# ACT copies the attention sums out of PSUM, and DVE takes their reciprocal out of SBUF in two halves

## The chip, the cores and the metric

The kernel runs on one core of a Trainium2 chip. The time is device time in microseconds (us) of one execution; lower is better. The engines are PE (matrix products), DVE (vector), ACT (activations and copies), POOL (a second, slower vector engine) and SP, whose queue issues the kernel's DMA transfers. PE writes its results to PSUM, which DVE and ACT can read; POOL and the DMAs here work on SBUF and on main memory.

## The reference

One layer of a bidirectional encoder is computed for two sequences, `prompt` (1024 tokens) and `sample` (2048 tokens), with the same weights. Three groups of heads work beside each other on one input projection; the change lies in the two that are attention.

```python
def block_self_attention(q, k, v):          # 8 heads of 64, keys shared by 4 heads
    def one_block(qblk):
        s = jnp.einsum('bqkgd,bskd->bkgqs', qblk, k) * scale
        p = jax.nn.softmax(s, axis=-1)
        return jnp.einsum('bkgqs,bskd->bqkgd', p, v)
...
def memory_attention(q, k, v):              # 4 heads, 256 memory tokens
    s = jnp.einsum('bthd,bmhd->bhtm', q, k) * (D ** -0.5)
    p = jax.nn.softmax(s, axis=-1)
    return jnp.einsum('bhtm,bmhd->bthd', p, v)
...
    mix = jnp.concatenate([pool_out, attn_out, x_out], axis=-1)   # each times its silu gate
    y = jnp.einsum('bte,ed->btd', mix, w_out)
    return x + rms_norm(y, norm_post)
```

All values are float32.

## The kernel before

A first stage (up to about 700 us) normalises the inputs, makes the projections and writes q, k, v and gates to main memory. The second stage is attention, output projection and final norm; the change is in it.

**Groups.** The second stage takes 256 queries at a time, a `Pair`: eight pairs of `sample`, then four of `prompt`. Each pair has three `Group`s: kind 0 and kind 1 are self-attention over all keys (16 chunks of 128 keys in sample, 8 in prompt), kind 2 is attention over the memory (2 chunks). Their order is 0, 2, 1 (2, 0, 1 in the first pair): 36 groups, the last three of them after all others of the prompt.

**Slots.** The main loop runs over `slots`, one for each chunk of each group. In a slot, PE makes the scores of a chunk in two halves into S (`weights`, two PSUM buffers), ACT takes their exponential into P, DVE (and in sample POOL for the first 512 columns) adds P up over the chunks into z (`sums`), and `largest` looks ahead: it makes scores of a later group into a PSUM tile N, and DVE reduces that to its maximum. Products of P with V go into one PSUM tile `acc` (`values`, four chunks at a time), and pieces of the output projection of an earlier pair fill gaps on PE.

**The end of a group.** `at(slot, f)` puts work into a slot: with a whole number it stands between the two halves of `weights`, with + END (0.5) at the slot's end. Say that the group's last chunk is over and count the slots behind it as k = 0, 1, 2 and so on; they are those of the next groups.
- end of k=1, `totals`: PE adds z over the partitions, into a tile `zt` of the same pool as N. This pool (`psn`) has two buffers.
- k=2, `take`: DVE multiplies `acc` with the gate, into o.
- end of k=2, `inverse`: DVE takes the reciprocal of `zt` into rz; SP sends four rows of rz to main memory (`rows`) and then back, spread over 64 partitions each, as gz (two transfers).
- end of k=5 at the earliest, `mix_out`: POOL multiplies o by gz. Two slots' order later (k=7, between the halves) ACT rounds it into `mix`, and at the end of k=7 POOL makes the low part of `mix`. In a pair's kind-1 group this comes at once; for its other two groups a hold (`HOLD`) puts it many slots later.

**What sets the order.** PE, ACT, DVE and POOL run the instructions in the order in which this code issues them. SP's queue is not in that list: the scheduler puts the transfers in order. Every queue is worked off in its order, and an instruction that waits holds all behind it. Where each N stands is also decided when the kernel is built: the two buffers alternate, but in k=2 and k=3 behind each `zt` two tiles of `largest` follow each other in the one that `zt` does not hold, and that of k=4 comes into `zt`'s.

Line numbers: `largest` reduces N in line 194 and multiplies in 183 and 191; scores S are 220 and 224, their exponential 227; sums 239 (POOL) and 240 (DVE); values 252; totals 260; take 266; reciprocal 272; `rows` 274; gz 278; POOL's product o 288; `mix` 416; the transpose of the maxima 128 and the four small transfers of its rows into qb 209.

Of the kernel before, what the change touches and what calls it, by code (L numbers as in the profile page):

```python
# [7 lines left out]
F32 = mybir.dt.float32  # L8
# [15 lines left out]
def encoder(ctx, tc, I, O):  # L24


    nc = tc.nc
# [105 lines left out]
    class Group:  # L133
# [132 lines left out]
            nc.vector.tensor_tensor(out=self.o, in0=self.acc,  # L266
                                    in1=self.gate.rearrange("p i t q -> p (i t q)"), op=ALU.mult)

        def inverse(self):

            r = dbl.tile([128, 256], F32, name="rz", tag="rz", bufs=1)
            nc.vector.reciprocal(out=r, in_=self.zt[:, 0:256])  # L272
            rows = dram.tile([4, 256], F32, name="rows", tag="rows", bufs=4)
            nc.sync.dma_start(out=rows, in_=r[0:128:32])
            self.gz = dbl.tile([128, 512], F32, name="gz", tag="gz")
            for j in range(2):
                src = rows[2 * j:2 * j + 2].rearrange("l q -> (l q)").unsqueeze(0)
                nc.sync.dma_start(out=self.gz[64 * j:64 * j + 64], in_=src.broadcast_to([64, 512]))
# [13 lines left out]
    class Pair:  # L292
# [15 lines left out]
        def pool(self, slot):  # L308
            self.mix = [own.tile([128, NC, 2, 128], F32R, name="mix", tag=f"mix{hl}") for hl in range(2)]
            store_mix(slot, self, 0, self.u.rearrange("p c q -> p (c q)"),  # L310
                      self.g.rearrange("p c t q -> p (c t q)"))
# [96 lines left out]
    END = 0.5  # L408

    def at(slot, f, *args):  # L410

        later.setdefault(slot, []).append((f, args))
# [24 lines left out]
    for g in groups:  # L437
        n, c = first[g], g.chunks
        at(n + END, g.load_late)
        for k in range(0, c, RUN):  # L440
            ks = list(range(k, min(k + RUN, c)))
            at(n + ks[-1] + 1 + END, g.values, ks)
        at(n + c + 1 + END, g.totals)
        at(n + c + 2, g.take)
        at(n + c + 2 + END, g.inverse)
    for c in range(NC):
        at(4 + 3 * c, load_w_out, c)
        at(7 + 3 * c, split_w_out, c)
# [4 lines left out]
    looks, n = {}, len(slots)  # L453
# [406 lines left out]
    dbl = pool("p2two", 2)  # L860
# [14 lines left out]
    with tc.manual_schedule(engines=order):  # L875
        slot = 0
        while slot < len(slots) or later or fill:
            g, k = slots[slot] if slot < len(slots) else (None, 0)
# [13 lines left out]
            n = -(-(len(fill) - pauses) // max(1, until[0] - slot - pauses)) if fill else 0  # L892
            for _ in range(n):
                x = fill.pop(0)
                if x is None:
                    break
                out, h, c, start, final = x
# [57 lines left out]
```

## Time and profile before

| | us |
|---|---|
| median of 3 runs | 1884.36 |
| lowest and highest | 1883.71, 1887.12 |
| profiled execution, its own time | 1885.09 |
| profiled execution, span | 1883.0 |
| PE busy in the span | 1816.8 |
| DVE, ACT, POOL busy | 1131.4, 697.3, 856.7 |

The profile gives one execution. "Busy" is the time in which an engine runs instructions; a wait is idle time of an engine just before an instruction, put down to what ended it. The granted clock of PE is 1.00 at full speed and 0.50 at half; its mean here is 0.991. In a timeline row stand start, duration, engine, line, operation and tiles, and in brackets the idle time before it with what ended it; "x2" is two merged instructions.

### The profile page before, as it was taken

How to read it: one execution, taken by the hardware profiler on the slowest of the kernel's cores; microseconds unless marked ns; L12 is line 12 of the kernel's file. 1: busy time of each engine (PE TensorE's matmuls, PEld its weight loads, DVE VectorE, ACT ScalarE, POOL GpSimd, SP SyncE). 2: the span in 40 equal slices, each digit the busy share in tenths (PEclk: the TensorE clock that was granted, in tenths of full speed). 3: DMA queues.
4: the chain of work that ended last, by engine and by line, in shares of the span. 5: the costliest groups of instructions: out<-in, count | busy, mean ns of one | idle time of the engine just before them, and what ended most of it. 6: DMA issues, size and time to landing. Idle time of an engine off the chain costs nothing. (4 is left out here: it accounts for less than half of the span.)

```text
span 1883.0 us, 23531 instructions
## 1 busy us (share of the span) xinstructions
PE 1816.8 (96%) x8520; PEld 1282.0 (68%) x8520; DVE 1131.4 (60%) x1304; ACT 697.3 (37%) x1266; POOL 856.7 (45%) x756
## 2 busy tenths in 40 slices
PE   7999999999999998999999999999999999999996
PEld 6888888988988874465564656556565656565564
DVE  7755146431545167867768676767868576756743
ACT  5523233222422115434434343444434343433331
POOL 3665017520546008845638374664837461413313
PEclk9999999999999999999999999999999999999998
DMA  7634454254433926212122220212222242223211
GB/s 243 201 113 121 109 160 132 76 162 110 116 113 102 216 70 167 68 30 79 46 79 62 70 64 25 79 45 79 62 74 62 67 132 64 91 84 100 86 40 62
DMA packets 148485, 181.83 MB, mean 97 GB/s; under 512 B 21505, under 2 KB 118417, under 8 KB 148369
## 3 DMA queue, kind: packets, MB, share of 16 engines
q1 hardware_dynamic: 148368, 180.33, 33.6%
q8 instruction: 67, 1.10, 0.3%
q14 instruction: 50, 0.40, 0.1%
HBM read 126.50 MB, written 53.62 MB: 96 GB/s over the span
## 5 line engine op out<-in xcount | busy, mean ns | idle before, releaser
L227 ACT ACTIVATE P<-S 128x512 f32<-128x512 f32 x688 | 399.3, 598 | 558.3 <-PE S L220 436.2
L194 DVE TENSOR_REDUCE nb<-N 128x1 f32<-128x1024 f32 x256 | 311.6, 1218 | 240.3 <-PE N L191 239.5
L239 POOL TENSOR_TENSOR z<-z,P 128x512 f32<-128x512 f32 x224 | 316.9, 1415 | 223.7 <-ACT P L227 218.8
L252 PE MATMUL acc<-P,V 128*64 128x512 f32 (+1 forms) x1472 | 320.8, 578 | 0.5
L220 PE MATMUL S<-qa,KA 128*128 128x512 f32 x640 | 275.0, 430 | 9.2 <-ACT P L227 9.2
L240 DVE TENSOR_TENSOR z<-z,P 128x512 f32<-128x512 f32 (+1 forms) x272 | 273.6, 1006 | 12.7 <-ACT P L227 12.3
L63 POOL TENSOR_TENSOR rs<-rs,mhalf 128x1 f32<-128x1 f32 (+2 forms) x100 | 100.4, 1007 | 386.2 <-DVE rs L61 386.1
L220 PE MATMUL S<-qb,KB 65*128 65x512 f32 x640 | 254.5, 398 | 0.0
L548 PE MATMUL pz<-hT_hi,w_hi 128*128 128x512 f32 x592 | 233.2, 394 | 1.4 <-ACT vmst L806 0.8
L549 PE MATMUL pz<-hT_lo,w_hi 128*128 128x512 f32 x592 | 232.3, 392 | 0.0
L550 PE MATMUL pz<-hT_hi,w_lo 128*128 128x512 f32 x592 | 232.1, 392 | 0.2 <-DVE w_lo L69 0.2
L191 PE MATMUL N<-KA,qa 128*128 128x512 f32 x640 | 208.1, 406 | 18.4 <-DVE rz L272 11.7
L252 PEld LDWEIGHTS acc<-P,V 128*64 128x64 f32 x1472 | 98.6, 138 | 180.3 <-issue 171.2
L220 PEld LDWEIGHTS S<-qa,KA 128*128 128x128 f32 x640 | 120.4, 188 | 143.6 <-issue 72.5
L194 DVE TENSOR_REDUCE top<-N 128x1 f32<-128x1024 f32 (+1 forms) x88 | 107.0, 1218 | 96.7 <-PE N L191 76.9
L191 PEld LDWEIGHTS N<-KA,qa 128*128 128x128 f32 x640 | 116.9, 191 | 61.7 <-DVE nb L194 22.1
L548 PE MATMUL pz<-w_hi,hT_hi 128*128 128x384 f32 (+1 forms) x416 | 140.3, 338 | 1.4 <-ACT hT_hi L68 1.4
L549 PE MATMUL pz<-w_lo,hT_hi 128*128 128x384 f32 (+1 forms) x416 | 139.9, 336 | 1.0 <-DVE w_lo L69 0.9
L550 PE MATMUL pz<-w_hi,hT_lo 128*128 128x384 f32 (+1 forms) x416 | 140.1, 338 | 0.0
L357 PE MATMUL py<-wo_hi,mix 128*128 128x512 f32 x352 | 137.7, 391 | 0.0
L358 PE MATMUL py<-wo_lo,mix 128*128 128x512 f32 x352 | 137.6, 391 | 0.0
L359 PE MATMUL py<-wo_hi,mix 128*128 128x512 f32 x352 | 137.4, 390 | 0.0
(116 smaller groups left out, 2487.9 us busy)
## 6 DMA issues: line engine op xcount, KB each, us to landing
wraw<-w_in SPq DMA_DIRECT2D x15, 1536.0 KB
dg<-gst SPq DMA_DIRECT2D x48, 256.0 KB
qa<-dq SPq DMA_DIRECT2D x48, 256.0 KB
gz<-rows SPq DMA_DIRECT2D x72, 128.0 KB
x<-x_sample SPq DMA_DIRECT2D x16, 512.0 KB
xr<-x_sample SPq DMA_DIRECT2D x16, 512.0 KB
y_sample<-xr SPq DMA_DIRECT2D x16, 512.0 KB
dq<-qst SPq DMA_DIRECT2D x96, 64.0 KB
```

The source lines that it names most:

```text
L191: nc.tensor.matmul(S[:, 512 * b:512 * b + 512], lhsT=q, rhs=KA[self.kind][:, k:k + 512], start=True, stop=True)
L194: nc.vector.tensor_reduce(out=out, in_=S, axis=AX.X, op=ALU.max, negate=True)
L220: nc.tensor.matmul(S, lhsT=K[self.kind][rows_, keys], rhs=q, start=n == 0, stop=n == 1)
L227: nc.scalar.activation(out=self.P[k][:, j], in_=S, func=AF.Exp)
L239: nc.gpsimd.tensor_tensor(out=z[:, :cut], in0=a[:, :cut], in1=P[:, :cut], op=ALU.add)
L240: nc.vector.tensor_tensor(out=z[:, cut:], in0=a[:, cut:], in1=P[:, cut:], op=ALU.add)
L252: nc.tensor.matmul(self.acc[64 * j:64 * j + 64, x], lhsT=v, rhs=P[:, j, x], start=(k, i) == (0, 0), stop=k == self.chunks - 1, skip_group_ ...
L357: nc.tensor.matmul(ps, lhsT=mh, rhs=wo_hi[:, c, cols], start=first, stop=False)
L358: nc.tensor.matmul(ps, lhsT=mh, rhs=wo_lo[:, c, cols], start=False, stop=False)
L548: nc.tensor.matmul(ps, lhsT=sh, rhs=mh, start=c == 0, stop=False)
L549: nc.tensor.matmul(ps, lhsT=sh, rhs=ml, start=False, stop=False)
L550: nc.tensor.matmul(ps, lhsT=sl, rhs=mh, start=False, stop=c == n - 1)
```

## The change

`inverse` is cut in two. A new step `take_sums` in k=2 has ACT copy the 128 x 256 sums out of `zt` into an SBUF tile zs. At the end of k=2 DVE takes the reciprocal of the first 128 columns out of zs, and at the end of k=3 that of the other 128. Only then `rows` and gz are sent. zs and rz have one buffer each.

```diff
-        def inverse(self):
-
-            r = dbl.tile([128, 256], F32, name="rz", tag="rz", bufs=1)
-            nc.vector.reciprocal(out=r, in_=self.zt[:, 0:256])
+        def take_sums(self):
+
+            self.zs = dbl.tile([128, 256], F32, name="zs", tag="zs", bufs=1)
+            self.rz = dbl.tile([128, 256], F32, name="rz", tag="rz", bufs=1)
+            nc.scalar.copy(out=self.zs, in_=self.zt[:, 0:256])
+
+        def inverse(self, half):
+
+            r, t = self.rz, self.zs
+            x = slice(128 * half, 128 * half + 128)
+            nc.vector.reciprocal(out=r[:, x], in_=t[:, x])
+            if half == 0:
+                return
             rows = dram.tile([4, 256], F32, name="rows", tag="rows", bufs=4)
             nc.sync.dma_start(out=rows, in_=r[0:128:32])
...
         at(n + c + 1 + END, g.totals)
         at(n + c + 2, g.take)
-        at(n + c + 2 + END, g.inverse)
+        at(n + c + 2, g.take_sums)
+        at(n + c + 2 + END, g.inverse, 0)
+        at(n + c + 3 + END, g.inverse, 1)
```

With it the built program lets the two buffers of N alternate throughout: the tile of k=2 stands beside `zt`, that of k=3 in `zt`'s buffer, that of k=4 again in the other. PE's and POOL's own order is unchanged.

DVE, behind a kind-1 group of the prompt; z are the sums, N the look-ahead's scores, top and rows the maxima and their transpose. Before:

```order
L266 TENSOR_TENSOR o<-acc,gate 128x512
L272 RECIPROCAL rz<-N 128x256
L240 TENSOR_TENSOR z<-z,P 128x1024
L194 TENSOR_REDUCE top_5434<-N 128x4
L128 STREAM_TRANSPOSE rows_13825<-top_5434 128x32
L240 TENSOR_TENSOR z<-z,P 128x1024
```

And with the change (its lines behind 272 have moved by up to 11):

```order
L266 TENSOR_TENSOR o<-acc,gate 128x512
L279 RECIPROCAL rz<-zs 128x128
L240 TENSOR_TENSOR z<-z,P 128x1024
L194 TENSOR_REDUCE top_5434<-N 128x4
L128 STREAM_TRANSPOSE rows_13909<-top_5434 128x32
L279 RECIPROCAL rz<-zs 128x128
L240 TENSOR_TENSOR z<-z,P 128x1024
```

The second half stands behind a sum, a reduction and, here, the transpose.

SP's queue at the same place; qb<-rows are the four small transfers of the transposed maxima. Before:

```order
L173 DMA gate<-dg_1_3_74 128x2x128 x2
L274 DMA rows<-rz 4x256
L278 DMA gz<-rows 64x512 x2
L209 DMA qb<-rows_13825 1x8x32 x4
L209 DMA qb<-rows_13870 1x8x32 x4
```

With the change:

```order
L173 DMA gate<-dg_1_3_74 128x2x128 x2
L209 DMA qb<-rows_13909 1x8x32 x4
L283 DMA rows<-rz 4x256
L287 DMA gz<-rows 64x512 x2
L209 DMA qb<-rows_13960 1x8x32 x4
```

`rows` and gz now stand behind the first four of these transfers. So it is behind the kind-1 groups of the last sample pair and of the first three prompt pairs; behind the other sample pairs' kind-1 groups no transfer has changed its place.

ACT behind the same group, P<-S being exponentials, two to a slot. Before:

```order
L416 CAST mix<-o 128x512 x2
L227 ACTIVATE P<-S 128x512 x14
L416 CAST mix<-o 128x512
L227 ACTIVATE P<-S 128x512 x5
L365 COPY y<-py 128x512
```

With the change:

```order
L425 CAST mix<-o 128x512 x2
L227 ACTIVATE P<-S 128x512 x4
L273 COPY zs<-N 128x256
L227 ACTIVATE P<-S 128x512 x10
L425 CAST mix<-o 128x512
L227 ACTIVATE P<-S 128x512 x5
```

The copy stands after the first exponential of k=2; the rounding of `mix` for this group stands where it stood, ten exponentials later.

## Prediction

> **What bounds the kernel now.** I began with the page's busy shares, then read who waits for whom on the tensor engine, and then the order of time around single groups.
>
> ```profile
> PE 1816.8 (96%) x8520; PEld 1282.0 (68%) x8520; DVE 1131.4 (60%) x1304; ACT 697.3 (37%) x1266; POOL 856.7 (45%) x756
> ```
>
> PE is the bound: 66 us of the 1883.0 us span are all it does not work. A change that touches DVE and ACT can bring only what PE waits for them. For the buffers N, which `largest` and `totals` share, that is:
>
> ```profile
> PE N L191 <- DVE rz L272: 11.7, 13, 2.0
> PE N L191 <- DVE nb L194: 5.8, 16, 1.0
> PE N L183 <- DVE top L194: 2.1, 4, 0.6
> ...
> PE N L191 <- DVE rz L272: 5.2, 9, 0.6
> ...
> PE N L191 <- DVE rz L272: 5.9, 3, 2.0
> PE N L183 <- DVE top L194: 1.8, 3, 0.6
> ```
>
> The columns are us in total, times, longest. The first three rows are the whole run, the fourth is 700 to 1550 us (sample; all of the nb row falls there too), the last two 1580 to 1800 us (prompt). Together 19.6 us, 1.04% of the run; no more than that can be won from idle PE. I count slots from the end of a group: k=0 is the first slot of the group behind it. In k=2 and k=3 both `largest` tiles must use the one N that `zt` does not hold (the nb and top waits), and the one of k=4 waits for the reciprocal (rz). Of the nb row about 1.1 us (its longest and one of 0.2) lie elsewhere. So the sample groups offer 5.2 + 4.7 = 9.9 us, the last sample group 0.6 + 0.3 = 0.9, three of the prompt's four kind-1 groups 5.9 + 1.8 = 7.7 (behind the fourth there is no group).
>
> **The work itself.**
>
> ```profile
> L272 DVE RECIPROCAL rz<-N 128x256 f32<-128x256 f32 x36 | 62.9, 1748 | 4.4 <-PE N L260 3.6 <-DMA rows<-rz 0.8
> L609 ACT COPY z<-pz 128x256 f32<-128x256 f32 x24 | 9.3, 386 | 0.0
> ```
>
> The change adds 36 ACT copies. The trace has the same form, PSUM to SBUF: 386 ns, 13.9 us in all, on an engine that is 37% busy. A half reciprocal out of SBUF is not in the trace. Below, half of 1748 is 874 ns; above, a whole one. 6.8 ns an element says that the time is in the elements, so I take 0.9 us: DVE loses 36 x 0.05 = 2 us, off the path. Both ends matter little: at 1.7 us each DVE would lose 30 us of its 750 idle.
>
> **Sample groups: a gain.** A kind-1 group, k=2 to k=8, engine by engine:
>
> ```profile
> 909.65 1.75 DVE L272 RECIPROCAL rz<-N 128x256 f32<-128x256 f32 x1
> 911.31 0.63 DVE L240 TENSOR_TENSOR z<-z,P 128x512 f32<-128x512 f32 x1
> 911.86 1.21 DVE L194 TENSOR_REDUCE nb<-N 128x1 f32<-128x1024 f32 x1
> ...
> 907.49 0.60 ACT L227 ACTIVATE P<-S 128x512 f32<-128x512 f32 x1 [0.69 <-PE S L220]
> 919.35 1.19 ACT L227 ACTIVATE P<-S 128x512 f32<-128x512 f32 x2 [0.29 <-PE S L220]
> 920.43 0.61 ACT L416 CAST mix<-o 128x512 fp32r<-128x512 f32 x1
> ...
> 916.71 1.29 POOL L288 TENSOR_TENSOR o<-o,gz 128x512 f32<-128x512 f32 x1 [3.63 <-DMA gz<-rows]
> ...
> 909.19 0.73 PE L191 MATMUL N<-KA,qa 128*128 128x512 f32 x2 [0.31 <-DVE nb L194]
> 911.45 0.73 PE L191 MATMUL N<-KA,qa 128*128 128x512 f32 x2 [0.60 <-DVE rz L272]
> 921.64 0.47 PE L220 MATMUL S<-qa,KA 128*128 128x512 f32 x1
> ...
> 862.61 0.73 PE L191 MATMUL N<-KA,qa 128*128 128x512 f32 x2 [0.36 <-DVE nb L194]
> ```
>
> The copy stands behind the exponential of 907.49: done at 908.1 + 0.4 = 908.5, before the N of k=3 could start (909.19 - 0.31 = 908.9). That N now goes into zt's buffer, the next one into the buffer that L194 cleared at 909.1; both waits go, 0.91 us. The copy falls into ACT's pauses; without them it would cost at most 36 x 0.4 us.
>
> What comes later is gz. The second half stands behind L240 and L194: 909.65 + 0.9 + 0.6 + 1.2 + 0.9 - overlaps = 913.1, where the whole one ended at 911.4. So `rows`, gz and POOL's o move by 1.7 us, to 918.4; o ends at 919.7. ACT's mix, pulled ahead with PE to 919.5, waits 0.2, and the exponential behind it holds the S of 921.64 (now 920.7) by 0.15. A kind-1 group keeps 0.76 of 0.91 us; a kind-2 group keeps its 0.36 (last row), since its o comes many slots after its gz. Seven kind-1 groups lose 7 x 0.15 = 1.1: the sample side gains 9.9 - 1.1 = **8.8 us**. Bounds: 0, if ACT is late with the copy, to 9.9.
>
> **Prompt groups: the gain goes, and more may.** The order shows that in the last four kind-1 groups before the final one (one sample, three prompt) the four transfers qb<-rows now stand ahead of `rows` on SP. The first prompt one:
>
> ```profile
> 1632.20 0.69 DVE L266 TENSOR_TENSOR o<-acc,gate 128x512 f32<-128x512 f32 x1 [1.28 <-POOL mix L416]
> 1632.81 1.75 DVE L272 RECIPROCAL rz<-N 128x256 f32<-128x256 f32 x1
> 1636.80 0.21 DVE L128 STREAM_TRANSPOSE rows<-top 128x32 f32<-128x32 f32 x1
> ...
> 1630.97 0.74 PE L183 MATMUL N<-KA,qa 128*128 128x256 f32 x4 [0.59 <-DVE top L194]
> 1634.61 0.73 PE L191 MATMUL N<-KA,qa 128*128 128x512 f32 x2 [1.97 <-DVE rz L272]
> 1646.53 0.39 PE L224 MATMUL S<-qa,KA 128*128 128x256 f32 x2
> ...
> 1634.58 0.56 SPq L274 DMA_DIRECT2D rows<-rz  x1
> ...
> 1639.89 1.62 POOL L288 TENSOR_TENSOR o<-o,gz 128x512 f32<-128x512 f32 x1 [6.49 <-DMA gz<-rows]
> ...
> 1645.12 0.61 ACT L416 CAST mix<-o 128x512 fp32r<-128x512 f32 x1
> ...
> L209 SPq DMA_DIRECT2D qb<-rows x144: 623/632/791, 688.5 to 1795.5; - x144
> ```
>
> DVE's take is held by POOL (1.28), not by PE, so this chain keeps its place in time. The transpose ends 0.85 earlier, at 1636.2; four issues of 0.63 and the pauses between them take SP to 1638.95; then `rows`, 4.4 us later than 1634.58. From `rows` to o passed 5.3 us: o starts at 1644.3, ends at 1645.6 to 1645.9, and the mix moves from 1645.12 to 1645.9. PE has by then won 2.6 us and stands still for it: the exponential behind the mix ends at 1647.0, the S of 1646.53 starts then. The 2.6 us are gone and 0.5 is lost. With the same 4.4 us the other three follow from:
>
> ```profile
> 1568.43 1.29 POOL L288 TENSOR_TENSOR o<-o,gz 128x512 f32<-128x512 f32 x1 [11.39 <-DMA gz<-rows]
> 1715.27 1.27 POOL L288 TENSOR_TENSOR o<-o,gz 128x512 f32<-128x512 f32 x1 [8.07 <-DMA gz<-rows]
> 1788.87 1.27 POOL L288 TENSOR_TENSOR o<-o,gz 128x512 f32<-128x512 f32 x1 [6.87 <-DMA gz<-rows]
> ...
> 1571.39 0.61 ACT L416 CAST mix<-o 128x512 fp32r<-128x512 f32 x1
> 1719.92 0.61 ACT L416 CAST mix<-o 128x512 fp32r<-128x512 f32 x1
> 1794.86 0.61 ACT L416 CAST mix<-o 128x512 fp32r<-128x512 f32 x1
> ```
>
> o would end at 1574.1, 1720.9 and 1794.5: the mix moves by +2.7, +1.0 and -0.4; less 0.3 of slack as in the first, PE by +2.4, +0.7, -0.7. The four sum to **+2.9 us**; bounds: -8.6 (nothing is late, 0.9 and 7.7 are won) to +8 (o another 1.3 us later in each, a quarter of the 5.3 from `rows` to o).
>
> **The clock.**
>
> ```profile
> 1632.07:1635.48 3.41, 1.45 (x7) 0.82 (x5) 3.28 (x3) 1.08 (x2) 1.33 (x2) 1.00 0.88 282
> 1635.48:1638.89 3.41, 3.41 (x10) 0.99 (x10) 3.38 (x5) 0.60 (x1) 0.00 (x0) 0.50 0.32 99
> 1703.75:1707.16 3.41, 2.11 (x10) 1.16 (x9) 2.13 (x3) 2.17 (x4) 3.41 (x3) 1.00 0.49 171
> 1707.16:1710.57 3.41, 2.17 (x6) 1.33 (x8) 3.40 (x3) 0.06 (x1) 0.04 (x1) 0.50 0.70 212
> ```
>
> Stretches of 3.41 us, PE busy first, granted clock in the third column from the right: after one with PE busy for 1.45 or 2.11 of 3.41 the next is granted half. The old waits paid that before the mix, where it now lies under the wait. The new one, over 2 us without work, is paid behind it: 3.41 us at half clock is 1.5 to 1.7 us, 1.5 to 2.6 a group with a second stretch partly idle. I take 1.5, as behind 1635.48: 4 x 1.5 = **+6.0 us** (0 to 10.4). The Trainium skill, "TensorE: Matmul & The Clock Gate", Part 1, has half rate come after at least one idle window of about 3.4 us. The rows above, halved with PE busy for 42% and 62% of the window, speak against waiting for a whole one.
>
> The tail stays: its `rows` come after both halves back to back, 0.1 us later, beside PE work that lasts longer.
>
> **The sum.** -8.8 + 2.9 + 6.0 = +0.1 us on the profiled run's own 1885.09 us (span 1883.0), so 1885.2. The median of the three runs lies 0.7 below the profiled one: 1884.5.
>
> **The rivals.**
> - The idle PE costs no clock behind the mix: -8.8 + 2.9 = -5.9, about 1878.5. The rule of the Trainium skill above would give this case, since no wait here lasts 3.4 us. For it: where a wait falls in its stretch is chance, and a wait cut in two by a border may be too short on both sides. Against: behind both old waits shown above the clock was halved. 14%.
> - gz is not late enough to hold ACT in the last four: -8.8 - 0.9 - 7.7 = -17.4, about 1867. It needs o about 2 us earlier than I reckon. For it: the mix has 3.6 us of slack at 1639.89. Against: four issues on one queue cannot shrink. 12%.
> - Slower: `rows` and gz, sent behind four small transfers, land later still. Each us more is paid in full in the four groups, and idles PE long enough for a second half-clock stretch: +4 x (1.1 + 1.1) = +8.8, about 1893. For it: no row shows these transfers behind four others. Against: the four are small. It decides from half a us a group: 0.5 x 4 + a second stretch in two is past +3.8. 19%.
> - The change does not free N sooner, because ACT comes late to the copy: no 8.8, but the late gz: +8.9, about 1893. Against it speak ACT's pauses. 5%.
>
> **How the numbers follow.** The forecast holds 50%, of which 42 lie within 0.2% (3.8 us; about what a measurement of this kernel can tell from no change), 4 faster and 4 slower. Faster: 4 + 14 + 12 = 30%; slower: 4 + 19 + 5 = 28%. The range goes from the no-clock case, less 4.5 for gz being earlier than reckoned in two of the four groups, to the slower rivals, 1874 to 1894; the 12% of the second rival and a few above stay out. The forecast's own range is 1879 to 1889.
>
> **What would show it.** Right: the waits of N for rz gone and those for nb and top down to about 1 us; a new wait of ACT mix for POOL o in four groups near 1573, 1645, 1720 and 1794 us, 2 to 5 us each, and S waiting for ACT P there; half clock behind each. Wrong: POOL o less than 3 us later there (faster), mix waits above 1 us in the sample groups too, or N waiting for ACT zs (slower).

## The result, and the profile after

| | before | changed |
|---|---|---|
| median, us | 1884.03 | 1900.88 |
| lowest and highest, us | 1882.67, 1887.12 | 1899.89, 1902.86 |
| profiled execution, own time and span, us | 1885.09, 1883.0 | 1902.86, 1901.1 |

The changed kernel is slower by 0.9%: ratio 1.0086, interval 1.0074 to 1.0098, four runs of each. The prediction was 1884.5 us with a range up to 1894; it held no change for the likeliest.

The page's busy row of the changed kernel, and below it who waits for whom on PE (us in total, times, longest):

```profile
PE 1822.7 (96%) x8520; PEld 1283.9 (68%) x8520; DVE 1136.6 (60%) x1340; ACT 707.8 (37%) x1302; POOL 854.9 (45%) x756
...
PE S L220 <- ACT P L227: 21.1, 38, 1.5
PE S L224 <- ACT P L227: 15.1, 6, 5.7
...
PE N L191 <- DVE top L194: 4.8, 8, 0.8
...
PE N L191 <- DVE nb L194: 1.0, 1, 1.0
```

The same two rows of S in the kernel before:

```profile
PE S L220 <- ACT P L227: 9.2, 31, 0.5
...
PE S L224 <- ACT P L227: 1.7, 3, 1.2
```

The wait of N for the reciprocal (11.7 us) is gone, and the waits of N for L194 have fallen from 7.9 to 5.8: the change does what it says, and N waits 13.8 us less. The 4.8 us that are left for top are not the old ones: all eight lie between 1557 and 1825 us, where PE, which now comes earlier, waits for DVE's reductions. In place of the old waits PE waits 25.3 us more for the exponentials that free S. And though PE executes the same 8520 instructions, it is busy 5.9 us longer: more of its work ran at half clock. What the exponentials stand behind on ACT shows in the groups by line, first of before, then of the changed kernel:

```profile
L416 ACT CAST mix<-o 128x512 fp32r<-128x512 f32 x36 | 21.5, 619 | 25.5 <-POOL o L288 25.4
```

```profile
L279 DVE RECIPROCAL rz<-zs 128x128 f32<-128x128 f32 x72 | 67.2, 937 | 7.9 <-ACT zs L273 6.0 <-DMA rows<-rz 2.0
...
L425 ACT CAST mix<-o 128x512 fp32r<-128x512 f32 x36 | 21.6, 620 | 50.7 <-POOL o L297 50.5
L273 ACT COPY zs<-N 128x256 f32<-128x256 f32 x36 | 13.2, 367 | 1.2 <-PE N L260 1.2
```

`mix` waits twice as long for POOL's product with gz, 50.5 us instead of 25.4. The copy costs 0.37 us each and half a reciprocal 0.94, close to the 0.39 and 0.9 of the prediction.

**Where the time went.** I cut both traces at the `totals` of each group and compared the 36 stretches. Each holds the same work. In the sample a stretch grows by PE's idle time, by half of the PE work that ran at half clock, and by about 0.26 us more for each wait of PE (below). Totals of the differences, changed minus before; the prediction's 8.8 us of the sample are split by its own rows:

| stretches behind | predicted, us | measured, us | of it idle PE |
|---|---|---|---|
| first two groups (sample) | -1.3 | -1.3 | -0.7 |
| 6 sample kind-2 groups | -2.2 | -3.6 | -2.0 |
| 7 sample kind-1 groups | -5.3 | **+5.5** | +2.3 |
| last sample and first three prompt kind-1 groups | +8.9 | **+15.4** | +10.1 |
| first three prompt kind-2 groups | 0 | **+2.4** | +2.4 |
| all other, first stage too | 0 | -0.3 | +0.1 |
| sum | +0.1 | +18.1 | +12.2 |

**A sample kind-1 group.** Timeline rows of the changed kernel behind the totals of 903.38 us (start, duration, engine, line, operation; idle time before it in brackets):

```profile
906.99 1.29 POOL L239 TENSOR_TENSOR z<-z,P 128x512 f32<-128x512 f32 x1 [0.18 <-ACT P L227]
907.79 1.03 DVE L240 TENSOR_TENSOR z<-z,P 128x512 f32<-128x512 f32 x1
...
909.88 0.94 DVE L279 RECIPROCAL rz<-zs 128x128 f32<-128x128 f32 x1
910.84 0.56 SPq L283 DMA_DIRECT2D rows<-rz  x1
...
916.20 1.82 POOL L297 TENSOR_TENSOR o<-o,gz 128x512 f32<-128x512 f32 x1 [6.25 <-DMA gz<-rows]
916.20 0.68 DVE L240 TENSOR_TENSOR z<-z,P 128x512 f32<-128x512 f32 x1
...
918.05 0.62 ACT L425 CAST mix<-o 128x512 fp32r<-128x512 f32 x1 [1.60 <-POOL o L297]
...
919.22 0.50 PE L220 MATMUL S<-qa,KA 128*128 128x512 f32 x1 [1.50 <-ACT P L227]
```

The chain is the one that the prediction followed, second half, `rows`, gz, o, mix, exponential, S; but it ends 1.5 us too late, not 0.15. It starts too late already: the second half ends 7.44 us behind totals, where the prediction's sum gives 7.0 (913.1 less 906.10), because DVE's sum between the halves, beside a sum of POOL that began 0.8 us ahead of it, takes 1.03 us and not 0.63. Two pairs later, other rows of the same work:

```profile
1135.33 1.28 POOL L297 TENSOR_TENSOR o<-o,gz 128x512 f32<-128x512 f32 x1 [6.10 <-DMA gz<-rows]
1135.45 1.71 DVE L240 TENSOR_TENSOR z<-z,P 128x512 f32<-128x512 f32 x1
...
1137.81 0.50 PE L220 MATMUL S<-qa,KA 128*128 128x512 f32 x1 [0.84 <-ACT P L227]
```

Here POOL starts 0.12 us ahead of DVE's sum and takes 1.28 us, while DVE takes 1.71 instead of 0.68; in the first rows they start together (3 ns apart) and POOL is the one that takes 0.54 longer. In the twelve traces on record, 32 such pairs of POOL's o and a sum of DVE start within 0.2 us of each other, and in all of them one takes its usual time and the other 1.64 to 1.82 us; where the starts are more than 3 ns apart, it is the earlier one that keeps its time. The Trainium skill, "SBUF — State Buffer", section "SBUF: two separate sides", has the two engines share a pair of ports that goes whole to the one that starts first; these pairs agree with that. Here 0.1 us in the arrival of gz so decides over 0.5 us of o, and with it over PE's wait, 1.50 or 0.84 us.

**The clock.** Clock stretches of 3.41 us (length, PE busy first, granted clock third from the right) around the first of these waits, around a third one, of 1.51 us, which begins at 1028.17, and in the first prompt kind-1 group:

```profile
916.20:919.62 3.42, 1.92 (x9) 1.04 (x7) 2.24 (x4) 1.82 (x4) 3.34 (x3) 1.00 0.00 0
919.62:923.03 3.41, 3.41 (x10) 1.01 (x10) 2.01 (x3) 0.63 (x2) 3.41 (x3) 0.50 0.00 0
...
1025.44:1028.85 3.41, 2.73 (x12) 1.70 (x10) 3.04 (x4) 1.53 (x3) 2.11 (x2) 1.00 0.05 16
1028.85:1032.27 3.42, 2.59 (x12) 1.07 (x14) 2.42 (x3) 1.86 (x4) 3.34 (x3) 1.00 0.00 0
1032.27:1035.68 3.41, 3.41 (x18) 1.73 (x13) 0.51 (x1) 0.65 (x2) 3.33 (x3) 1.00 0.00 0
1650.07:1653.48 3.41, 0.73 (x2) 0.30 (x2) 2.90 (x3) 0.49 (x1) 1.85 (x1) 1.00 0.08 22
1653.48:1656.89 3.41, 2.73 (x8) 1.46 (x10) 2.75 (x2) 1.71 (x4) 1.27 (x1) 0.50 0.83 215
1656.89:1660.31 3.42, 3.42 (x10) 0.95 (x8) 0.28 (x1) 0.00 (x0) 0.00 (x0) 0.50 0.00 0
```

A wait of 1.50 us inside one stretch halves the next (1.7 us lost); one of 1.51 us that a border cuts in two (2.73 and 2.59 busy) halves nothing. The time from the first totals to the next grew from 53.88 to 55.91 us, that of the group with the cut wait from 53.90 to 54.25. Three of the seven sample kind-1 groups were halved so. In the prompt group the wait of 2.67 us halves the next stretch, and because that one holds another 0.68 us of idle PE, the one behind it too: 6.15 us of work at half clock, 3.1 us lost, where the prediction took one stretch and 1.5. Behind the last of the four late groups PE stands still for 5.67 us, the longest wait of the row S L224 above; three stretches from 1807.08 on are at half clock there, the first without any work in it, and 5.90 us of work fall into the other two.

**A prompt kind-1 group.** The rows around that wait:

```profile
1642.83 0.91 DVE L279 RECIPROCAL rz<-zs 128x128 f32<-128x128 f32 x1
1642.94 2.76 SPq L209 DMA_DIRECT2D qb<-rows  x4
...
1645.80 0.53 SPq L283 DMA_DIRECT2D rows<-rz  x1
...
1651.11 1.85 POOL L297 TENSOR_TENSOR o<-o,gz 128x512 f32<-128x512 f32 x1 [10.98 <-DMA gz<-rows]
...
1652.99 0.62 ACT L425 CAST mix<-o 128x512 fp32r<-128x512 f32 x1 [4.63 <-POOL o L297]
...
1654.16 0.79 PE L224 MATMUL S<-qa,KA 128*128 128x256 f32 x2 [2.67 <-ACT P L227]
```

The half is done at 1643.74, and `rows`, which stands behind the four transfers, leaves 2.06 us later. From the take (1638.91; before 1632.20) `rows` is 4.5 us later than before, as forecast (4.4).

**A prompt kind-2 group.** Rows of the changed kernel, then of before:

```profile
1601.82 0.94 DVE L279 RECIPROCAL rz<-zs 128x128 f32<-128x128 f32 x1
...
1606.48 1.28 DVE L392 SCALAR_TENSOR_TENSOR y<-y,rs,npost 128x1024 f32<-128x1024 f32 x1 [0.66 <-POOL rs L63]
...
1610.32 0.59 ACT L374 COPY y<-py 128x512 f32<-128x512 f32 x1 [6.42 <-POOL xr L395]
...
1611.45 0.50 PE L220 MATMUL S<-qa,KA 128*128 128x512 f32 x1 [1.35 <-ACT P L227]
```

```profile
1599.70 1.28 DVE L383 SCALAR_TENSOR_TENSOR y<-y,rs,npost 128x1024 f32<-128x1024 f32 x1 [0.66 <-POOL rs L63]
...
1603.54 0.58 ACT L365 COPY y<-py 128x512 f32<-128x512 f32 x1 [5.62 <-POOL xr L386]
...
1604.68 0.50 PE L220 MATMUL S<-qa,KA 128*128 128x512 f32 x1 [0.54 <-ACT P L227]
```

Totals stand at 1601.03 and 1595.04. The second half of the kind-0 group (1601.82) comes ahead of the output norm on DVE, whose y is 5.45 us behind totals, not 4.66; POOL adds y to xr, ACT's copy waits for that, the exponentials for the copy, and S is 0.8 us later. DVE is 60% busy, but here it has no slack.

### The profile page after: what moved, and what is told of

Read it like the earlier page. It is cut to its first block, busy times and chain, and to the rows that moved or that the text cites. A ratio compares the mean times of both kernels' runs of the same rounds, so it can differ in the third digit from the quotient of the medians.

```text
span 1901.1 us, 23674 instructions
## 1 busy us (share of the span) xinstructions
PE 1822.7 (96%) x8520; PEld 1283.9 (68%) x8520; DVE 1136.6 (60%) x1340; ACT 707.8 (37%) x1302; POOL 854.9 (45%) x756
## 5 line engine op out<-in xcount | busy, mean ns | idle before, releaser
L194 DVE TENSOR_REDUCE nb<-N 128x1 f32<-128x1024 f32 x256 | 311.6, 1218 | 237.4 <-PE N L191 236.6
L252 PE MATMUL acc<-P,V 128*64 128x512 f32 (+1 forms) x1472 | 329.8, 592 | 0.9 <-DVE o L266 0.4
L194 DVE TENSOR_REDUCE top<-N 128x1 f32<-128x1024 f32 (+1 forms) x88 | 106.9, 1218 | 99.5 <-PE N L191 79.5
```

The source lines that it names most:

```text
L194: nc.vector.tensor_reduce(out=out, in_=S, axis=AX.X, op=ALU.max, negate=True)
L252: nc.tensor.matmul(self.acc[64 * j:64 * j + 64, x], lhsT=v, rhs=P[:, j, x], start=(k, i) == (0, 0), stop=k == self.chunks - 1, skip_group_ ...
```

## The experiments

Each changes the changed kernel, but for e8; ratios are against the kernel before, run beside it on the same chip. In each batch of runs the kernel before stood between 1883.8 and 1885.6 us.

**e1_whole: the copy without the delay.**

```diff
-        def inverse(self, half):
+        def inverse(self):
...
-            x = slice(128 * half, 128 * half + 128)
-            nc.vector.reciprocal(out=r[:, x], in_=t[:, x])
-            if half == 0:
-                return
+            nc.vector.reciprocal(out=r, in_=t)
...
-        at(n + c + 2 + END, g.inverse, 0)
-        at(n + c + 3 + END, g.inverse, 1)
+        at(n + c + 2 + END, g.inverse)
```

> The copy by ACT stays, the reciprocal is taken whole out of SBUF at the end of k=2, and rows and gz are sent there, as before. Late-gz theory (the changed kernel loses because gz comes later, so that ACT's mix, the score behind it and PE wait, and PE pays half clock behind each wait): all that remains is the earlier release of N. Sample: 6 kind-2 groups -0.6 us each, 7 kind-1 groups about -1.2, the first pair -1.6; prompt: three kind-1 groups -2.5 and a half-clock stretch of 1.7 less each. Together -20, about 1864 us (1858 to 1872), no wait of mix for POOL o above 0.5 us behind a kind-1 group. Copy theory (the copy or the new order of the N buffers costs): 1884 us or more, with the sample kind-1 groups longer than before. Halves theory (DVE loses by the two instructions): 1875 to 1884.

Measured: 1863.83 us, ratio 0.9892 (0.9873 to 0.9910). The copy is no cost but a gain of 1.1%. The sample kind-1 groups came to -9.6 us, the kind-2 groups to -3.7, the four late ones to -6.4. PE's waits for N and S:

```profile
PE S L220 <- ACT P L227: 9.7, 31, 0.8
PE N L191 <- DVE top L194: 5.3, 7, 1.2
...
PE S L224 <- ACT P L227: 1.9, 3, 1.2
```

The waits of S are back at before's. Those of N for the reciprocal stay gone; the 5.3 us for top are those of the late groups again. Mix waited for o behind no kind-1 group of the sample, and in the prompt for 0.58 and 0.75 us behind two of them, a little over the expected 0.5.

**e2_no_copy: the delay without the copy.**

```diff
-            self.zs = dbl.tile([128, 256], F32, name="zs", tag="zs", bufs=1)
...
-            nc.scalar.copy(out=self.zs, in_=self.zt[:, 0:256])
...
-            r, t = self.rz, self.zs
+            r, t = self.rz, self.zt
```

> No copy: both halves read the sums out of PSUM, the second a slot later, and rows and gz are sent behind it. Late-gz theory: gz is as late as in the changed kernel, and N is now held a slot longer than before, so three tiles of largest follow each other in one buffer: no gain in the kind-2 groups, and longer waits of N for DVE; 1903 to 1925 us. Copy theory: without the copy the time falls back to 1886 us or below.

Measured: 1931.98 us, ratio 1.0254 (1.0231 to 1.0276), past the upper end of what was expected. N is now the wait:

```profile
PE N L191 <- DVE nb L194: 28.6, 30, 2.0
PE N L191 <- DVE top L194: 13.7, 8, 3.4
```

Three tiles in one buffer cost more than I had reckoned, also because every sample kind-1 group now has a half-clock stretch (30.0 us of work in the seven, 15 us lost). Without the copy it is worse, not better; as N is also held longer here, it is e1, which gains with the copy, that makes the copy theory fall.

**e3_mix_later: the late gz, with its reader moved behind it.**

```diff
-            wait = max(first[g] + g.chunks + 5, free)
+            wait = max(first[g] + g.chunks + (6 if g.kind == 1 else 5), free)
```

> The changed kernel, with POOL's o, ACT's mix and POOL's low part of a kind-1 group put one slot later (1.5 us in the sample, about 2 in the prompt). Late-gz theory: in the sample mix's wait of 0.9 to 1.6 us goes, with the half-clock stretches behind it (8 x 1.0 + 3 x 1.7 = 13 us); in the last sample group and the three prompt groups the wait of 2.66 us shrinks by 1.5 to 2.2 us and at least one of two half-clock stretches goes (4 x 3 = 12 us at most): 1875 to 1888 us. Copy and halves theories: gz is not what is waited for; 1898 to 1903 us.

Measured: 1863.83 us, ratio 0.9889 (0.9869 to 0.9909), below what was expected. In the sample's kind-1 groups mix no longer waits. Behind the last four it still does, for 2.4 us in three and 4.5 in the last; in the first prompt group:

```profile
1631.21 0.62 ACT L425 CAST mix<-o 128x512 fp32r<-128x512 f32 x1 [2.41 <-POOL o L297]
```

But no S waits for the exponential behind it, except for 1.38 us in the last group, and no half-clock stretch stood behind any of the eleven. The three prompt kind-2 groups stayed at +0.8 us each. The halves and their late gz are all still there; what has changed is that almost nothing that PE needs stands behind them.

**e4_prompt_k2: the delay in the sample alone.**

```diff
-        at(n + c + 3 + END, g.inverse, 1)
+        at(n + c + (3 if g.s else 2) + END, g.inverse, 1)
```

> The changed kernel, but in the prompt's groups both halves stand at the end of k=2 with rows and gz behind them; the sample's groups stay as changed. Late-gz theory: the three prompt kind-1 groups lose what they had lost against before (3.9, 3.0 and 3.0 us) and win up to 2.5 us each beyond it, the three prompt kind-2 groups lose their 0.8 us each (the second half no longer stands ahead of the y chain on DVE): 12 to 20 us less, 1881 to 1889 us. Halves theory (two instructions where one was): no more than 3 us less, 1897 to 1901 us.

Measured: 1875.93 us, ratio 0.9964 (0.9947 to 0.9980), 23 to 25 us below the changed kernel (by the ratios and by the medians) instead of 12 to 20; its ten runs spread from 1874.2 to 1886.5. The profiled one is the slowest of them, with 3.5 us of that in the first stage, so I read its groups: the prompt kind-2 groups are back at 0.0, and the three prompt kind-1 groups at -1.9, -0.3 and -3.1 us against before, 15.1 less than in the changed kernel. The sample kind-1 groups stand at +4.4. That the spread comes from where waits of about 1.5 us fall against the borders of the clock's stretches fits its trace (two of seven halved), but other runs left no trace to show it.

**e7_whole_k3 and e10_halves_k2: whole or halves, k=2 or k=3.** e7 takes the whole reciprocal at the end of k=3, e10 both halves at the end of k=2:

```diff
-        at(n + c + 2 + END, g.inverse)
+        at(n + c + 3 + END, g.inverse)
```

```diff
-        at(n + c + 3 + END, g.inverse, 1)
+        at(n + c + 2 + END, g.inverse, 1)
```

(the first against e1, the second against the changed kernel)

> The copy by ACT, and the whole reciprocal in one instruction at the end of k=3: not halved, but as late as the second half. Late-gz theory: gz comes another 0.8 us later than in the changed kernel, mix waits 1.8 to 2.4 us in the sample's kind-1 groups (with a half-clock stretch behind more of them) and 0.8 us more in the last four; the prompt kind-2 groups lose 1.6 us instead of 0.8: 1905 to 1925 us. Halves theory (two instructions are what costs): 1865 to 1885 us.

> The copy by ACT and both halves, one behind the other, at the end of k=2, rows and gz behind them. Of the four ways (whole or halves, k=2 or k=3) this is the fourth. If the slot counts: as with the whole reciprocal at k=2, 1862 to 1867 us (DVE spends 0.1 us more a group, off the path). If the two instructions count: 1885 us or more.

Measured: e7 1896.8 us, ratio 1.0067 (1.0049 to 1.0085); e10 1864.04 us, ratio 0.9891 (0.9870 to 0.9912). So the four are

| | k=2 | k=3 |
|---|---|---|
| whole | 1863.8 | 1896.8 |
| halves | 1864.0 | 1900.9 |

The slot makes 33 to 37 us, the cut 0 to 4. At k=3 these 4 us are a sum of larger differences that cancel: by the traces, e7's sample kind-1 groups are 10.4 us shorter than the changed kernel's, its last four 7.0 shorter, and its three prompt kind-2 groups 10.2 longer. e7 was below my range, and its trace says why. The same group as above:

```profile
908.78 1.74 DVE L278 RECIPROCAL rz<-zs 128x256 f32<-128x256 f32 x1
...
910.55 0.56 SPq L280 DMA_DIRECT2D rows<-rz  x1
...
915.81 1.29 POOL L294 TENSOR_TENSOR o<-o,gz 128x512 f32<-128x512 f32 x1 [5.58 <-DMA gz<-rows]
...
917.14 0.62 ACT L422 CAST mix<-o 128x512 fp32r<-128x512 f32 x1 [0.57 <-POOL o L294]
```

Its `rows` leaves not 0.8 us later than with halves but 0.4 earlier (7.05 us behind totals at 903.50, there 7.46): with no first half in k=2, the sum and the reduction ahead of it on DVE are done sooner. That is enough for o to miss DVE's sum (1.29 us) and for mix to wait 0.57 instead of 1.60, with no half clock: its sample kind-1 groups come to -4.9 us. Its prompt kind-2 groups, with a whole reciprocal ahead of the norm, have 2.4 us of idle PE each against before, where 1.6 were expected; two of the three pay half clock on top and are 5.1 us longer.

**e9_qb_pool: SP's order.**

```diff
-                nc.sync.dma_start(out=row[:, :, b].bitcast(F32), in_=r[32 * b:32 * b + 8])
+                (nc.gpsimd if (self.s, self.kind) == (0, 2) else nc.sync).dma_start(out=row[:, :, b].bitcast(F32), in_=r[32 * b:32 * b + 8])
```

> The changed kernel, with the four small transfers qb<-rows of the prompt's kind-2 groups issued by POOL instead of SP: these are the ones that stand ahead of rows in the last sample and the first three prompt kind-1 groups, where rows waited 2.0 us for them behind the end of the second half. SP-order theory (a part of the late gz): rows, gz and o come 2.0 us earlier in these four, mix's wait and PE's 2.66 us shrink by as much, to under the 1.3 us from which PE was halved, so most of the two half-clock stretches (up to 3.1 us each) goes too: 1880 to 1893 us. If the queue's order does not matter there: 1898 to 1903 us.

Measured: 1883.02 us, ratio 0.9981 (0.9969 to 0.9992). The first prompt group:

```profile
1639.74 0.91 DVE L279 RECIPROCAL rz<-zs 128x128 f32<-128x128 f32 x1
1640.11 2.15 POOL L209 DMA_DIRECT2D qb<-rows  x4 [3.09 <-DVE rows L128]
1640.68 0.55 SPq L283 DMA_DIRECT2D rows<-rz  x1
```

`rows` follows the half at once. The four stretches came to -3.6 us against before instead of +15.4, and only the last of them keeps a half-clock stretch, all with DVE, ACT and PE in an unchanged order. So 2 us of waiting on a queue made 19 us by the traces, more than the changed kernel's whole loss of 16.9.

**e11_ahead_of_N: the same slots, an earlier place on DVE.**

```diff
-        at(n + c + 3 + END, g.inverse, 1)
+        at(n + c + 3 - 0.25, g.inverse, 1)
...
+            due(slot - 0.25)
             if slot in looks:
                 looks[slot][0].largest(looks[slot][1])
```

> The changed kernel with the same instructions in the same slots; only, in k=3, the second half stands ahead of the reduction of N (and of the transpose) on DVE instead of behind it, so that rows also stands ahead of the four qb transfers on SP again. Late-gz theory: gz and o come about 1.2 us earlier in the sample's kind-1 groups (o near 11.6 us behind totals instead of 12.7 to 12.9) and 3 to 4 us earlier in the last four; mix waits for neither, the half-clock stretches behind it go, only the 0.8 us of the three prompt kind-2 groups stay: 1864 to 1872 us. If it is the spreading over two slots as such that costs: 1890 us or more. The reduction comes 0.9 us later, and N may wait for it in k=5: up to 0.5 us a group, 10 us in all, if so.

Measured: 1869.45 us, ratio 0.9928 (0.9910 to 0.9945). o starts 11.5 to 11.7 us behind totals in six of the seven sample kind-1 groups (11.6 was expected), and they come to -8.8 us. A miss: the 0.8 us of the prompt kind-2 groups went too. Another: behind the last four mix still waits 0.1 to 1.1 us, and PE waits longer for the reduction that now stands behind the half, as in the first prompt group:

```profile
1633.67 0.73 PE L191 MATMUL N<-KA,qa 128*128 128x512 f32 x2 [1.57 <-DVE top L194]
```

In e1 the same wait is 0.82 us. Three of the four keep a half-clock stretch, and together they come to -2.3 us, where e1's come to -6.4. Still, what costs is not the spreading over two slots, but which instructions stand ahead of the second half.

**e8_before_mix_later and e6_whole_mix_later.** e8 is the kernel before with e3's edit, e6 is e1 with it.

> The kernel before, with the kind-1 groups' o and mix one slot later and nothing else changed. Late-gz theory: before, mix waited for nothing behind a kind-1 group (idle 0.00), so its place a slot later brings nothing by itself: 1880 to 1888 us. If the later place is a gain of its own, and not one that meets the late gz: 1862 to 1875 us.

> The copy by ACT, the whole reciprocal out of SBUF at the end of k=2, and the kind-1 groups' o and mix one slot later. Late-gz theory: what the whole reciprocal leaves in the last two prompt groups (a wait of mix, a half-clock stretch) goes, and the 0.8 us of the three prompt kind-2 groups that the two halves cost when only mix was put later go too: 1858 to 1863 us. If mix has slack enough with the whole reciprocal, no change against it: 1863 to 1865 us.

Measured: e8 1884.89 us, ratio 0.9996 (0.9986 to 1.0005): no gain where gz is not late. e6 1860.03 us, ratio 0.9866 (0.9851 to 0.9881): the lowest median of all, 1.3% below before (its interval overlaps those of e1, e3 and e10), with no half-clock stretch behind any kind-1 group but the last.

Sample kind-1 groups side by side (the group of 903.38 in the changed kernel, the same group in the others); the first and third columns are us behind totals, the others us, "half clock" PE's work at half clock and "stretch" the time from these totals to the next:

| | o starts | o takes | mix | PE idle in the stretch | half clock | stretch |
|---|---|---|---|---|---|---|
| before | 10.61 | 1.29 | 14.33 | 0.91 | 0 | 53.88 |
| changed | 12.82 | 1.82 | 14.67 | 1.50 | 3.41 | 55.91 |
| e7 | 12.31 | 1.29 | 13.64 | 0.49 | 0 | 53.18 |
| e11 | 11.54 | 1.37 | 12.98 | 0.00 | 0 | 52.54 |
| e1 | 10.53 | 1.30 | 12.95 | 0.00 | 0 | 52.51 |

Without a wait mix comes 13.0 us behind totals, not the 13.4 that the prediction worked with (14.33 less 0.91); o must be ready by then.

## Why the prediction was wrong, point by point

- **The waits of N go, and the copy is hidden: right.** 13.8 us of N's waits went, ACT's copy took 0.37 us. e1 shows it alone.
- **What N's waits are worth: too small.** The prediction set a ceiling of 19.6 us, the idle PE that names N. e6 gained 25.6. A stretch behind a kind-1 group loses 0.91 us of idle in two waits and becomes 1.4 shorter (e1). The rest, 0.26 us a wait, is PE's own time by the profile: behind a wait the first two products of N take 0.73 us instead of 0.63 (at 906.00 and 907.47 in the changed kernel), and ahead of it the last product of S runs out alone, of which otherwise 0.16 us lie beside the next. Half-clock stretches that old waits had set off are on top. Idle time is no ceiling.
- **Sample kind-1 groups: the step that failed first.** The term was "loses only 0.15 of 0.91 us". The shift of gz was forecast at 1.7 us and was 2.0 to 2.4 (o from 10.5 to 10.7 us behind totals to 12.7 to 12.9), 0.4 of it the sum between the halves, which took 1.03 us and not 0.6; o ran into DVE's sum in four of seven, and PE had won 1.4, not 0.91, by then, so that mix was wanted earlier. Each is a few tenths; together they made waits of 0.84 to 1.51 us. And the clock, which the prediction charged to the last four groups alone, was halved behind three of them. +5.5 us came instead of -5.3: of the 18 us between forecast and result, 11 are here.
- **The last four groups: chain right, clock mis-sized.** PE worked 6.1, 6.2, 6.1 and 5.9 us at half clock behind the mix, 12.1 us lost in all, where 6.0 were taken and 10.4 was the upper bound. What is left of the 15.4, 3.3 us, is the late gz, forecast at 2.9: the mix came 2.7, 1.1, 0.2 and 0.2 us later behind totals, where 2.7, 0.8, 1.0 and -0.4 were forecast, so the sum fits better than its terms. The prediction had the second stretch among its slower rivals, but as the result of a later landing; from `rows` to o passed 5.3 us as before (1645.80 to 1651.11; 5.2 to 6.0 in the four, before 5.3 to 6.6), and in three of the four the second stretch followed a first one that held 0.7 us of idle PE.
- **"DVE loses 2 us, off the path": wrong at one place.** 0.8 us in each of three prompt kind-2 groups; e4, e7 and e11 show it go, treble and go with what stands ahead of the norm.
- **The rivals.** The slower one, "later landing", gave 1893 and had 19%; its sign was right, its mechanism only in part. The one in which gz is not late, 1867, is what e1 and e10 bring about by taking the delay away: 1864. "No clock cost" fell with the rows at 0.50, "N not freed sooner" with the rz row.
- **What would show it.** Most of the named signs were there: the rz row gone, mix waits of 4 to 5.3 us in the four groups, half clock behind each; but N's waits for nb and top are at 5.8 us, not at about 1. There was also the sign that the prediction called wrong and slower, mix waits above 1 us in the sample groups.

## What to carry to other kernels

When a change frees one buffer earlier and makes one result later, follow the later result to its last reader, and compare its arrival with the time at which the reader will want it after the gain, not before: each microsecond won upstream is taken from its slack. Count behind a moved instruction everything that its new place puts ahead of it on its own engine and on the queue that sends its result; here the later slot, with two such places on DVE and on SP, was worth 33 to 37 us, the cut into halves 0 to 4 in sum. And price a wait of PE from about 1.3 us on with the half-clock stretches that can follow it: 1.7 us each.

## What the runs showed of the hardware

- The changed kernel's stretches around the prompt kind-2 wait of 1.35 us:

```profile
1609.11:1612.52 3.41, 2.06 (x10) 1.36 (x9) 3.39 (x2) 2.20 (x6) 3.40 (x2) 1.00 0.37 154
1612.52:1615.94 3.42, 3.42 (x16) 2.80 (x15) 3.40 (x5) 1.07 (x2) 0.00 (x0) 1.00 0.01 1
```

PE busy for 2.06 of 3.41 us was not followed by half clock; 1.92 us was, but so was 2.11 us in the kernel before. A bound on PE's busy time alone does not separate them, but the doubtful band is narrow. In the twelve traces, from 720 us to shortly before the end, all 54 full-clock stretches with 1.54 us or more of idle PE were followed by half clock, 12 of 28 with 1.30 to 1.51 us, and 2 of 3809 with less (0.81 us in e1, 0.91 in e4). The Trainium skill, "TensorE: Matmul & The Clock Gate", Part 1, asks for an idle window of about 3.4 us. The measurement decides here: the waits that halved the clock in the sample's kind-1 groups lasted 1.50 us.
- A half-clock stretch that itself held 0.7 us of idle PE was followed by a second (three groups, 0.68 to 0.76 us); one fully busy was not. In the twelve traces all 25 half-clock stretches with 0.24 us or more of idle PE were followed by another, and none of the 68 with 0.11 us or less.
- POOL's product and DVE's sum, started within 0.12 us of each other, did not slow each other evenly: the first took its usual 1.28 or 0.68 us, the other 1.71 or 1.82.
- The reciprocal takes 1744 ns out of SBUF and 1748 out of PSUM for 256 columns, 937 for 128: the source makes no difference.
